# Hybrid decoder step on one core: a rest between the index groups, another first buffer for their relus, and a longer gap between attention's first loads and the values

## The chip, the core and the metric

The kernel runs on one core of a Trainium2 chip. The time is device time in microseconds (us) for one execution of the whole program, lower is better. TensorE (PE) does the matmuls, VectorE (DVE) and ScalarE (ACT) the element work, GpSimd (POOL) some element work and DMA issues, SyncE (SP) most DMA issues.

## What is computed

One step of a decoder layer for 1024 prompt tokens and 8 sample tokens: RMSNorm, one wide input projection, a sparse attention group (an index search picks 256 keys per query, attention then runs over these), an mLSTM group, and one output projection. The parts that the change touches are the index search and the attention over prompt tokens:

```python
def indexer_scores(qi, ki, wi):
    s = relu(einsum('bqhd,bld->bqlh', qi, ki))          # 16 heads of 64
    return einsum('bqlh,bqh->bql', s, wi) * IDX_SCALE

def block(args):                                         # one block of 128 queries
    scores = where(key_pos <= pos, indexer_scores(qib, ki, wib), -inf)
    _, idx = top_k(scores, 256)
    return sparse_attend(qb, k[idx], v[idx], idx <= pos)
```

## The kernel before

**Main work.** Nearly all of the span is a stream of projection matmuls on PE: first tile by tile (`mm`, L1596), then by a blocked scheme with fewer products (`product`, L1783; 48 matmuls of 258 columns each, every number split in a high and a low part so that three matmuls make one). Their inputs are weights that SP loads (L1768), ACT casts (L1771) and DVE subtracts (L1772), and partial sums that DVE evacuates (L1881) and SP stores and fetches (L1809, L1805).

**Side work.** The index search, attention, mLSTM and the sample tokens are generators ("jobs") in three lanes. Each `yield n` is n units of a job's weight. A lane hands its job's steps out evenly between the job's start and end (both in projection tiles; four clock steps make one), so a job's weight and a `yield` set the place of each step beside the projection, and a larger weight packs the other steps closer. A scheduler then puts the recorded instructions in an order on each engine by its own estimate of times; each engine runs its list in that order. The order is fixed when the program is built.

**Index search (`job_index`).** Query blocks 2 to 7 go in groups of two: (2,3), (4,5), (6,7). For each block and each of 16 heads PE makes scores (L483) in a PSUM bank, ACT applies the relu into one of three shared buffers "rl", "gt", "eq" (L486), and DVE adds the weighted relu to the block's sum s (L489; L497 and L499 for head 0). The buffers are taken in turn. Then a bit by bit search finds the 256th largest score (DVE L557 to L562, ACT L533, with gt and eq as scratch), and the mask is made in the same buffers: "gt" for the first block, "rl" for the second, with "eq" as scratch of both (L569 to L577). SP stores each mask to `biasS` (L578). A PSUM bank is free for another score when its relu is done; a buffer is free for a relu when DVE has read it and, if it held a mask, when the store has left it. At the border of two groups ACT, DVE, PE and SP so wait for each other in their own orders.

**Attention (`job_att`).** It opens its buffers in the space that the sample tokens' attention has left (its last store is L1438), loads the keys and the values (L605), the mask and the queries (L626, L628), rests for 15 units, transposes the values on PE (L613, eight transposes in two banks), splits values and queries (ACT L615, L633, DVE L616, L634), and then goes pair by pair through scores (L650), masked maximum (DVE L651), exp (ACT L667), transposes and values (L694, L703).

Of the kernel before, what the change touches and what calls it, by code (L numbers as in the profile page):

```python
# [42 lines left out]
T_AK = 9  # L43
T_AV = 11
T_AQ = 13
T_G = 21
# [131 lines left out]
def body(tc, A, stop=None):  # L178
# [270 lines left out]
    def job_index(groups):  # L449
        with tc.tile_pool(name="ix", bufs=2) as px:  # L450
# [4 lines left out]
            qv = qS.rearrange("(h p) r -> p h r", p=128)  # L455
            quads = [(i, h) for blocks in groups for i in blocks for h in range(0, 16, 4)]
            qis = {}
            ring, turn = ("rl", "gt", "eq"), [0]

            def load_q(n):  # L460
                if n < len(quads):
# [8 lines left out]
            yield 3000  # L470
            for blocks in groups:
                n = len(blocks)
                Sv = []
                for i in blocks:
                    W = (i + 1) * 128
# [88 lines left out]
                for q, i in enumerate(blocks):  # L564
                    W = (i + 1) * 128
                    gt = px.tile([128, S], BF16, name="rl" if q else "gt", bufs=1)
                    eq = px.tile([128, S], BF16, name="eq", bufs=1)
# [13 lines left out]
    def job_att():  # L581
        early.close()
        blocks = [(0, i) for i in range(7, -1, -1)] + [(1, i) for i in range(8)]
        pairs = [(g, i, hp) for g, i in blocks for hp in range(2)]
        with tc.tile_pool(name="at", bufs=2) as pa:
# [22 lines left out]
            def split_v(vt):  # L608
                vH, vL = (pa.tile([128, 8, 128], F32R, name=f"v{x}", bufs=1) for x in "HL")
                for b4 in range(2):  # L610
                    p = bank().rearrange("p (a b) -> p a b", a=4)
                    for j in range(4):
                        PE.transpose(p[:, j, :], vt[b4][:, j * 128:j * 128 + 128], ident)  # L613
                    bs = slice(b4 * 4, b4 * 4 + 4)
                    SC.copy(vH[:, bs], p)  # L615
                    V.tensor_tensor(vL[:, bs], p, vH[:, bs].bitcast(F32), OP.subtract)  # L616
                cur["v"] = vH, vL
                cur["rc"] = pa.tile([128, 4, 8], F32, name="rc", bufs=2)

            def load_q(g, i):  # L620
                W = (i + 1) * 128
                if i < 2:
                    bias = cmask[:, 256 - W:]
                else:
                    bias = pa.tile([128, S], BF16, name="bias", bufs=2)
                    SY.dma_start(bias[:, :W], biasS[i])  # L626
                q = pa.tile([128, 4, 128], F32R, name="qL", bufs=2)
                SY.dma_start(q.bitcast(F32), aqS[g].rearrange("(j p) r -> p j r", p=128)[:, :, i * 128:(i + 1) * 128])  # L628
                return q, bias
# [78 lines left out]
            split_k()  # L708
            vt = load_v(0)
            pre = load_q(*blocks[0])  # L710
            yield 15
            split_v(vt)
            split_q(*pre)
            pre = load_q(*blocks[1])
# [5 lines left out]
            for n, pair in enumerate(pairs):  # L720
                g, i, hp = pair
# [807 lines left out]
    def ix_weight(blocks):  # L1529
# [4 lines left out]
    groups = ((2, 3), (4, 5), (6, 7))  # L1534

    lanes = [Lane([Job("gates", 5, T_AK - 0.5, 14500, job_gates),
                   Job("index", T_AK + 2.1, 28.2, 6000 + sum(map(ix_weight, groups)), lambda: job_index(groups)),
                   Job("att", T_G + 17.8, 47.3, 2 * 2 * sum(2 * (1 + (i + 1) * 0.5) for i in range(8)) + 24, job_att, att_free),
                   Job("ml", T_G + 20, 55.8, 41, job_ml, lo_done)]),
             Lane([Job("prep", 3, T_AK + 1.8, 1 + 16 * 2, job_prep),  # L1540
                   Job("dscore", T_AK + 2.4, 17.9, 56 + 128 + 2, job_dscore),
# [593 lines left out]
    turn = [0]  # L2135
# [354 lines left out]
def build(arrays):  # L2490
    nc = bacc.Bacc("TRN2", target_bir_lowering=False, num_devices=1)
    A = {}
    for name, a in arrays.items():
        A[name] = nc.dram_tensor(f"in_{name}_dram", a.shape, mybir.dt.from_np(a.dtype), kind="ExternalInput").ap()
    for name, shape in OUTS.items():
        A[name] = nc.dram_tensor(f"out_{name}_dram", shape, F32, kind="ExternalOutput").ap()
    with tile.TileContext(nc, schedule_with_timeline_sim=True) as tc:
        body(tc, A)
    return nc
# [8 lines left out]
```

## Time and profile before

| | |
|---|---|
| median of 3 runs | 1910.79 us (1910.09 to 1913.55) |
| the profiled execution, its own time | 1910.03 us |
| its span, first to last instruction | 1908.2 us |
| PE busy | 1878.0 us, 98% of the span |
| weight load on PE | 1808.6 us, 95% |
| DVE busy | 1394.1 us, 73% |
| ACT busy | 915.0 us, 48% |
| POOL busy | 511.2 us, 27% |
| mean granted TensorE clock | 0.995 of full |

The profile is one execution. Busy times overlap, so that the span is about PE's busy time with PE's idle time. A line of the waits says which engine and line waited, for which engine and line, and gives the total, the number of times and the longest. A line of the timeline gives the start from the span's start, the length, the engine and line, the tiles, and in brackets the idle time before it with what ended it.

### The profile page before, as it was taken

The numbers are of one execution on the slowest core, as the hardware profiler recorded it, in microseconds if no ns is written. First come the engines' busy times: TensorE is split into PE (matmuls) and PEld (weight loads), VectorE is DVE, ScalarE is ACT, GpSimd is POOL, SyncE is SP. The second block draws the span as 40 slices with busy tenths as digits, with TensorE's granted clock in tenths as the row PEclk, the third lists the DMA queues.
The fourth block names the chain that finished last, engine by engine and source line by source line (L and its number), as shares of the span: only waits on it lengthen the run. The fifth ranks groups of instructions, "written<-read, shape, count | busy, mean of one in ns | idle before, by whom it ended". The sixth has DMA issues, their size and how long they took to land. (4 is left out here: it accounts for less than half of the span.)

```text
span 1908.2 us, 37435 instructions
## 1 busy us (share of the span) xinstructions
PE 1878.0 (98%) x13422; PEld 1808.6 (95%) x13422; DVE 1394.1 (73%) x3266; ACT 915.0 (48%) x1822; POOL 511.2 (27%) x600
## 2 busy tenths in 40 slices
PE   9999999999989999999999999999999999999998
PEld 8999999999989999999899999999999999987886
DVE  8564386776778988998566566558988676788786
ACT  8222145346445465522255555436656444454654
POOL 0599853320000011054111111102211241105541
PEclk9999999999999999999999999999999999999999
DMA  7577857757787798799977898688999979899797
GB/s 265 160 215 212 256 182 238 201 160 180 212 256 203 212 250 235 224 315 303 252 183 188 237 250 199 156 266 260 320 315 287 213 238 298 274 336 309 254 221 237
DMA packets 253703, 456.64 MB, mean 239 GB/s; under 512 B 38165, under 2 KB 113877, under 8 KB 249837
## 3 DMA queue, kind: packets, MB, share of 16 engines
q1 hardware_dynamic: 192445, 331.24, 53.5%
q0 software_dynamic: 27648, 102.34, 23.6%
q10 hardware_dynamic: 33424, 20.68, 3.6%
q8 instruction: 105, 1.72, 0.4%
q14 instruction: 81, 0.66, 0.1%
HBM read 363.72 MB, written 138.67 MB: 263 GB/s over the span
## 5 line engine op out<-in xcount | busy, mean ns | idle before, releaser
L1783 PE MATMUL pj<-xH 128*128 128x258 f32 x1920 | 546.7, 285 | 1.0 <-ACT mH L1581 1.0
L1783 PE MATMUL pj<-xL,xH 128*128 128x258 f32 x1920 | 546.0, 285 | 0.0
L1783 PE MATMUL pj<-xH,xL 128*128 128x258 f32 x1920 | 545.5, 285 | 0.0
L1783 PEld LDWEIGHTS pj<-xH 128*128 128x128 f32 x1920 | 363.7, 190 | 3.5 <-ACT mH L1581 1.4
L1783 PEld LDWEIGHTS pj<-xH,xL 128*128 128x128 f32 x1920 | 363.9, 190 | 1.7
L1783 PEld LDWEIGHTS pj<-xL,xH 128*128 128x128 f32 x1920 | 363.9, 190 | 1.5
L1596 PE MATMUL pj<-xH,wH 128*128 128x344 f32 (+1 forms) x816 | 265.3, 328 | 1.3 <-ACT xH L325 0.8
L1596 PE MATMUL pj<-xH,wL 128*128 128x344 f32 (+1 forms) x816 | 264.6, 325 | 0.5 <-DVE wL L269 0.5
L1596 PE MATMUL pj<-xL,wH 128*128 128x344 f32 (+1 forms) x816 | 264.5, 324 | 0.2 <-DVE xL L326 0.2
L269 DVE TENSOR_TENSOR wL<-wraw,wH 128x512 fp32r<-128x512 f32 (+2 forms) x151 | 117.4, 790 | 96.5 <-ACT wH L268 95.3
L268 ACT CAST wH<-wraw 128x512 fp32r<-128x512 f32 (+2 forms) x151 | 89.8, 607 | 181.8 <-PE pj L1596 102.5
L1596 PEld LDWEIGHTS pj<-xH,wH 128*128 128x128 f32 x816 | 153.0, 188 | 3.9 <-ACT xH L325 2.1
L1596 PEld LDWEIGHTS pj<-xL,wH 128*128 128x128 f32 x816 | 153.3, 188 | 1.1 <-DVE xL L326 0.7
L1596 PEld LDWEIGHTS pj<-xH,wL 128*128 128x128 f32 x816 | 153.3, 188 | 1.0 <-DVE wL L269 0.8
L2160 PE MATMUL pj<-wH,sH 128*128 128x512 f32 x336 | 131.8, 393 | 3.3 <-DVE yt L2278 2.9
L2160 PE MATMUL pj<-wH,sL 128*128 128x512 f32 x336 | 131.5, 391 | 0.0
L2160 PE MATMUL pj<-wL,sH 128*128 128x512 f32 x336 | 123.3, 392 | 0.5 <-DVE wL L2149 0.5
L1771 ACT CAST xH<-wH 128x1024 fp32r<-128x1024 f32 x91 | 75.9, 834 | 99.9 <-PE pj L1783 75.1
L1771 ACT CAST xH<-wL 128x1024 fp32r<-128x1024 f32 x91 | 76.1, 836 | 95.0 <-PE pj L1783 58.8
L1772 DVE TENSOR_TENSOR xL<-wH,xH 128x1024 fp32r<-128x1024 f32 x91 | 87.0, 956 | 15.6 <-ACT xH L1771 13.9
L1772 DVE TENSOR_TENSOR xL<-wL,xH 128x1024 fp32r<-128x1024 f32 x91 | 86.9, 955 | 11.4 <-ACT xH L1771 10.5
L1783 PE MATMUL bank<-xH 128*128 128x258 f32 x320 | 91.4, 286 | 0.0
(508 smaller groups left out, 4445.1 us busy)
## 6 DMA issues: line engine op xcount, KB each, us to landing
wraw<-in_wt_dram SPq DMA_DIRECT2D x144, 256.0 KB
usD<-in_wa_dram POOLq DMA_DIRECT2D x46, 512.0 KB, 7.8
wraw<-in_wa_dram SPq DMA_DIRECT2D x78, 256.0 KB
wraw<-in_wo_dram SPq DMA_DIRECT2D x64, 256.0 KB
usD<-in_wa_dram SPq DMA_DIRECT2D x26, 512.0 KB
wH<-in_wa_dram SPq DMA_DIRECT2D x25, 512.0 KB
wL<-in_wa_dram SPq DMA_DIRECT2D x24, 512.0 KB
spD<-ev SPq DMA_DIRECT2D x46, 258.0 KB
```

The lines of the kernel that those rows point to most:

```text
L268: a = paced("act", SC.copy(H[:, s, :cols], raw[:, s, :cols]))
L269: return a, V.tensor_tensor(L[:, s, :cols], raw[:, s, :cols], H[:, s, :cols].bitcast(F32), OP.subtract)
L1596: m = PE.matmul(ps[:cols, :cn], w_[:, k, :cols], x_[kk][:, c0:c0 + cn], start=(kk == ends[0] and z == 0), stop=(kk == ends[1] and z == 2))
L1771: paced("act", SC.copy(H[:, q], r))
L1772: paced("dve", V.tensor_tensor(L[:, q], r, H[:, q].bitcast(F32), OP.subtract))
L1783: PE.matmul(ps[c], w_[:, q, ks], x[y][:, c * CS:c * CS + CS], start=(first and q == 0 and k == 0 and z == 0), stop=(q == 1 and k == 3 and ...
L2160: PE.matmul(ps[b], S_[x][:, b * 128:b * 128 + 128], T_[y], start=(k == 0 and z == 0), stop=(k == 7 and z == 2))
```

## The change

It sets the turn of the relu buffers back to 0 at each group and turns their order to eq, gt, rl. It puts a rest of 7000 units ahead of the second and third group, and adds 14000 to the index job's weight. It makes the rest of attention between its first loads and the split of the values 24 units in place of 15, adds 9 to its weight, and moves its end from 47.3 to 47.5. No instruction of computation is added or taken away. The line numbers of the changed kernel are 3 higher from L475 on.

```diff
             quads = [(i, h) for blocks in groups for i in blocks for h in range(0, 16, 4)]
             qis = {}
-            ring, turn = ("rl", "gt", "eq"), [0]
+            ring, turn = ("eq", "gt", "rl"), [0]
...
             yield 3000
             for blocks in groups:
                 n = len(blocks)
+                turn[0] = 0
+                if blocks != groups[0]:
+                    yield 7000
                 Sv = []
...
             vt = load_v(0)
             pre = load_q(*blocks[0])
-            yield 15
+            yield 24
             split_v(vt)
...
-                   Job("index", T_AK + 2.1, 28.2, 6000 + sum(map(ix_weight, groups)), lambda: job_index(groups)),
-                   Job("att", T_G + 17.8, 47.3, 2 * 2 * sum(2 * (1 + (i + 1) * 0.5) for i in range(8)) + 24, job_att, att_free),
+                   Job("index", T_AK + 2.1, 28.2, 20000 + sum(map(ix_weight, groups)), lambda: job_index(groups)),
+                   Job("att", T_G + 17.8, 47.5, 2 * 2 * sum(2 * (1 + (i + 1) * 0.5) for i in range(8)) + 33, job_att, att_free),
```

**PE, start of the index search's third group.** In both programs the first four score tiles of the group stand some 200 projection matmuls earlier; these are the fifth and the sixth (bank is the PSUM bank, ki the index keys, qi the queries, the rest is projection). Before:

```order
L483 MATMUL bank<-ki_2323,qi 128x512
L483 MATMUL bank<-ki_2324,qi 128x512
L1783 MATMUL pj_5355<-xL,xH 128x258
L1783 MATMUL pj_5355<-xH,xL 128x258
L1783 MATMUL pj_5356<-xH 128x258
L483 MATMUL bank<-ki_2323,qi 128x384
L483 MATMUL bank<-ki_2324,qi 128x384
```

With the change:

```order
L486 MATMUL bank<-ki_2323,qi 128x512
L486 MATMUL bank<-ki_2324,qi 128x512
L1786 MATMUL pj_5356<-xL,xH 128x258
L1786 MATMUL pj_5356<-xH,xL 128x258
L1786 MATMUL pj_5356<-xH 128x258
L1786 MATMUL pj_5356<-xL,xH 128x258
L1786 MATMUL pj_5356<-xH,xL 128x258
L1786 MATMUL bank<-xH 128x258
L1786 MATMUL bank<-xL,xH 128x258
L486 MATMUL bank<-ki_2323,qi 128x384
L486 MATMUL bank<-ki_2324,qi 128x384
```

Counted in projection matmuls from the start of the program, the fifth tile stands after 2974 before and after 2983 with the change, the sixth after 2977 and after 2990. The first four stand after 2736 before, and after 2760 and 2784 (two each) with the change.

**SP, the stores of the second group's masks.** biasS_119 takes the mask of block 4 from gt, biasS_120 that of block 5 from rl; the other rows belong to the projection. Before:

```order
L1768 DMA wL<-in_wa_dram 128x1024
L578 DMA biasS_119<-gt 128x640
L1736 DMA xL<-xsD 128x516
L1768 DMA wH<-in_wa_dram 128x512
L1809 DMA spD<-ev 128x516
L1768 DMA wL<-in_wa_dram 128x512
L578 DMA biasS_120<-rl 128x768
```

With the change:

```order
L1771 DMA wL<-in_wa_dram 128x1024
L1739 DMA xL<-xsD 128x516
L1771 DMA wH<-in_wa_dram 128x512
L581 DMA biasS_119<-gt 128x640
L1812 DMA spD<-ev 128x516
L1771 DMA wL<-in_wa_dram 128x512
L581 DMA biasS_120<-rl 128x768
```

The store from gt has moved behind two loads of the projection; the one from rl stands where it stood.

**SP, attention's first loads.** attS is the last store of the sample tokens' attention, pP the buffers of the values. Before:

```order
L1438 DMA attS_107<-ot 128x4x8
L1438 DMA attS_108<-ot 128x4x8
L1768 DMA wH<-in_wa_dram 128x512
L605 DMA pP<-avS_101 128x512
L1809 DMA spD<-ev 128x516
L1805 DMA rstd<-spD 128x516
L1768 DMA wL<-in_wa_dram 128x512
L605 DMA pP<-avS_101 128x512
L626 DMA bias<-biasS_122 128x1024
L628 DMA qL<-aqS_104 128x4x128
```

With the change:

```order
L1441 DMA attS_107<-ot 128x4x8
L1441 DMA attS_108<-ot 128x4x8
L1812 DMA spD<-ev 128x516
L1808 DMA rstd<-spD 128x516
L608 DMA pP<-avS_101 128x512 x2
L1771 DMA wL<-in_wa_dram 128x1024
L629 DMA bias<-biasS_122 128x1024
L631 DMA qL<-aqS_104 128x4x128
```

The two loads of values now stand together and ahead of two weight loads that they followed, counting back from the 1024 wide wL. On PE the transposes of the values stand after 5736 and 5743 projection matmuls before (four each), and all eight after 5808 with the change. Attention's last value matmul stands after 7272 before and after 7296 with the change.

## Rows read from the trace of the kernel before

**Rows 1.** The page, part 1: busy us, share of the span, instructions.
```profile
PE 1878.0 (98%) x13422; PEld 1808.6 (95%) x13422; DVE 1394.1 (73%) x3266; ACT 915.0 (48%) x1822; POOL 511.2 (27%) x600
```

**Rows 2.** Waits of PE, whole span: total us, times, longest us.
```profile
PE bank L483 <- ACT gt L486: 5.6, 2, 4.8
PE pj L2160 <- DVE yt L2278: 2.9, 1, 2.9
PE bank L613 <- DMA pP<-avS: 2.4, 1, 2.4
```

**Rows 3.** Timeline of PE, third index group: start, length, instruction, idle before.
```profile
554.14 0.73 PE L483 MATMUL bank<-ki,qi 128*128 128x512 f32 x2 [1.54 <-ACT eq L486]
...
560.04 1.01 PE L483 MATMUL bank<-ki,qi 128*128 128x384 f32 x2 [4.80 <-ACT gt L486]
...
564.35 0.28 PE L1783 MATMUL bank<-xH 128*128 128x258 f32 x1
564.47 0.28 PE L1783 MATMUL bank<-xL,xH 128*128 128x258 f32 x1
```

**Rows 4.** Timeline of ACT, the same place.
```profile
553.49 0.60 ACT L486 ACTIVATE eq<-bank 128x512 f32<-128x512 f32 x1 [5.80 <-DVE rl L576]
559.49 0.49 ACT L486 ACTIVATE gt<-bank 128x384 f32<-128x384 f32 x1 [5.40 <-DMA biasS<-gt]
...
562.59 0.60 ACT L486 ACTIVATE rl<-bank 128x512 f32<-128x512 f32 x1 [0.31 <-DMA biasS<-rl]
```

**Rows 5.** Timeline of DVE, the masks of blocks 4 and 5.
```profile
547.58 0.32 DVE L577 TENSOR_SCALAR gt<-gt 128x640 bf16<-128x640 bf16 x1
...
552.85 0.55 DVE L576 TENSOR_TENSOR rl<-rl,eq 128x768 bf16<-128x768 bf16 x1
```

**Rows 6.** Timeline of SP's DMA queue, the same place.
```profile
547.68 0.33 SPq L1768 DMA_DIRECT2D wL<-in_wa_dram  x1
548.11 0.60 SPq L578 DMA_DIRECT2D biasS<-gt  x1
548.76 0.49 SPq L1736 DMA_DIRECT2D xL<-xsD  x1
549.35 0.41 SPq L1768 DMA_DIRECT2D wH<-in_wa_dram  x1
```

**Rows 7.** Windows: stretch, its us, busy by engine, PEclk, DMA share, GB/s.
```profile
550.00:555.00 5.00, 3.46 (x27) 3.17 (x25) 3.76 (x7) 0.60 (x1) 0.00 (x0) 1.00 1.05 279
555.00:560.00 5.00, 0.24 (x3) 0.03 (x1) 0.00 (x0) 0.49 (x1) 0.00 (x0) 0.73 0.93 320
560.00:564.20 4.20, 4.16 (x18) 4.17 (x19) 3.14 (x7) 2.36 (x4) 0.00 (x0) 0.50 0.37 112
```

**Rows 8.** DMA issues, whole span: count, KB each.
```profile
xL<-xsD SPq DMA_DIRECT2D x40, 258.0 KB
...
wH<-in_wa_dram SPq DMA_DIRECT2D x22, 256.0 KB
```

**Rows 9.** Timeline of PE, the transposes of attention's first values.
```profile
928.93 0.63 PE L613 MATMUL bank<-cst,pP 128*128 128x128 f32 x4 [0.94 <-DMA spD<-ev]
...
932.78 1.11 PE L613 MATMUL bank<-cst,pP 128*128 128x128 f32 x4 [2.39 <-DMA pP<-avS]
```

**Rows 10.** Windows, behind those transposes.
```profile
932.80:936.20 3.40, 3.40 (x16) 3.40 (x17) 0.82 (x2) 1.10 (x2) 0.63 (x1) 0.50 1.06 350
```

**Rows 11.** Timeline of SP's DMA queue, attention's first loads.
```profile
917.01 1.23 SPq L1438 DMA_DIRECT2D attS<-ot  x2
...
922.95 0.33 SPq L605 DMA_DIRECT2D pP<-avS  x1
...
925.98 0.91 SPq L605 DMA_DIRECT2D pP<-avS  x1
```

**Rows 12.** Waits of SP's DMA queue, 910 to 946 us.
```profile
SPq L605 <- DMA attS<-ot: 3.8, 2, 3.4
```

**Rows 13.** Windows: the stretch of attention.
```profile
937.00:1240.00 303.00, 302.28 (x2394) 295.24 (x2393) 188.50 (x513) 161.51 (x375) 35.43 (x41) 1.00 0.80 207
```

**Rows 14.** Windows: most of the third group's scores.
```profile
570.00:655.00 85.00, 85.00 (x622) 80.97 (x621) 75.92 (x158) 43.07 (x74) 7.58 (x11) 1.00 0.75 209
```

## Prediction, made before the changed kernel ran

> **What bounds the kernel.** I read the page's busy times first: PE is busy for 1878.0 us of a span of 1908.2 us, every other engine for 73% of it or less [rows 1]. So the bound is the stream of matmuls on PE, and the change neither adds to it nor takes from it. What an edit of order can win is PE's idle time, 30.2 us in all, and what idle time does to its clock. The waits of PE come next: the three longest lines are 5.6 us of index scores (L483) for a relu, 2.9 us in the output projection (L2160), and 2.4 us of attention's first transposes (L613) for a DMA [rows 2]. The change comes near the first and the third. The second lies far behind everything that moves, and I leave it as it is.
>
> At the third index group PE waits twice: 1.54 us until the relu into eq is done, and 4.80 us until the relu into gt is done [rows 3]. ACT shows why. The relu into eq began at 553.49, after DVE's last reading of eq in the mask of block 5; the relu into gt began at 559.49, when the store of block 4's mask had left gt [rows 4]. DVE had finished that mask by 547.9 [rows 5] and SP had issued its store at 548.11 [rows 6]: the store took 11.4 us, in a stretch in which the DMA engines were busy 93% of the time and more [rows 7]. The clock pays a second time. It was at full (2.4 GHz) before the wait, and 0.50 (1.2 GHz) from 560.0 to 564.2, in which PE was busy throughout [rows 7]: 4.2 us of work at half speed, 2.1 us lost. The place costs 1.54 + 4.80 + 2.1 = 8.4 us.
>
> At attention's start PE waits 0.94 us and then 2.39 us for the two loads of the values [rows 9], and runs the next 3.4 us at 0.50 [rows 10], 1.7 us lost. This place costs 0.94 + 2.39 + 1.7 = 5.0 us.
>
> **The change part by part: attention.** The loads were late because SP waited 3.4 us for the sample tokens' last store to leave the space [rows 12], issued the first load at 922.95 and the second at 925.98 [rows 11], and PE took them up 6.0 and 6.8 us after their issue [rows 9]. The rest of 24 units puts the transposes 72 and 65 projection matmuls later. One such matmul takes 0.12 us at full clock (from 564.35 to 564.47, [rows 3]), so that is 8.6 and 7.8 us. The loads themselves move forward in SP's order, together and ahead of two weight loads. The slack of over 7 us, against waits of 0.94 and 2.39 us, covers both, and without the waits I see no cause for the clock to fall there. I take -5.0 us; the ends are -3.3 (the clock falls anyway) and -5.0.
>
> What is queued behind them: SP still waits for the sample tokens' store, and now the 1024 wide weight load stands behind that wait. In the old order the 512 wide wL stood behind the same wait, 3.4 us [rows 12], and no wait of PE for a weight came of it; I cost this at nothing, covered by the weights already cast. If that cover were gone, it would cost the same 3.4 us.
>
> The rest of attention starts 72 matmuls later and ends 24 later, so it loses 48 x 0.12 = 5.8 us of some 300 us. In that stretch PE was busy 302.28 of 303 us and DVE 188.50, ACT 161.51 [rows 13]. DVE at 62% goes to some 63%; I cost this at nothing, with 0 and +5.8 as ends.
>
> **The index search.** The rest of 7000 of now 418,918 units is 1.14 of the 68.4 clock steps that the job has, and the other steps are packed 3.3% closer. At the second group it moves the first scores 36 projection matmuls back; Besides the 4.80 us only 0.8 us is left of that line's 5.6 [rows 2, 3], so that is worth nothing. At the third group it moves the first four score tiles by 24 and 48 matmuls. But these four wait in their banks in any case; PE stops at the fifth and the sixth, which need a bank back. Those move by 9 and 13 matmuls only.
>
> With the new turn the first relu goes into eq, the second into gt and the third into rl. The fifth tile then waits for the relu into eq, as before, behind the same reading of eq in block 5's mask, which ended at 553.4 [rows 5]. PE comes 9 x 0.12 = 1.1 us later, so of the 1.54 us some 0.5 us is left. The sixth tile waits for the relu into gt, **the same store as before**. If that store still left at 559.49, PE would have done 13 x 0.12 = 1.6 us more of its work by then, and the place would cost 1.6 us less. In the new order the store stands behind the loads of xL and wH, 258 and 256 KB [rows 8], which followed it before [rows 6]. At the 320 GB/s that the core moved there [rows 7] these 514 KB take 1.6 us. That gives back the whole gain. I take 0 for this part. The ends are -1.6, and +1.5: the gt store as late as the rl store, whose relu began at 562.59 [rows 4], which is 3.1 us later, less the 1.6.
>
> Here a rule of the Trainium skill speaks against the edit. The rows show only issue and release, 548.11 and 559.49 [rows 4, 6]. DMA: Bandwidth & Descriptors, section "Queues, rings and completion order", says that each DMA engine takes the descriptors of one queue in ring order. By that rule the store can't pass the two loads that now precede it, and the sum below holds; without it the sum would be 1.6 us lower. The trace doesn't contradict it: the relu into rl, whose store was issued later, was released later too. No run here isolates it.
>
> **Sum.** The profiled execution took 1910.03 us, 1.83 us of it outside its span. Less 5.0 for attention and 0 for the index search that is 1905.0 us. The median of the runs, 1910.79, lies 0.76 us above that execution, so I forecast 1905.8 us.
>
> **The rivals.** 0.2%, 3.8 us, is about what a measurement of this kernel can tell from no change; the bounds are 1907.0 and 1914.6 us.
>
> *Both places are cured.* The rest could hold the critical tiles back until the stores have left, or the stores could leave sooner because less is under way beside them. For it: the waits are named in the rows and the rest stands in front of just these scores. Against it: the tiles that stop PE move by about one us, where the store would have to come over 4 us earlier. It would give 1905.8 - 8.4 = 1897.4 us.
>
> *The index wait grows, or a new wait takes its place.* DMA was full, and the new order puts more in front of the store. At the upper end the store costs +1.5 us, and with another 3.4 us at half clock 1.7 us more: 1905.8 + 3.2 = 1909.0 us, no change to speak of. The same holds for one new wait of that size elsewhere, since most of the order of side work has moved by some matmuls.
>
> *Slower: DVE becomes the bound of the scores.* The rest takes its time from the other steps, and the scores come 3.3% closer. In the third group's scores DVE was already busy 75.92 of 85 us, 89% [rows 14]. Should DVE fall behind, relus wait for their buffers, scores for banks and PE for the scores. For the two groups behind a rest, at 85 us each, the price is 3.3% of 170 us, 5.6 us of waiting, and a fall of the clock at 1.7 us in each: 1905.8 + 9.0 = 1914.8 us. It decides from the point where 89% becomes 100%; 3.3% more makes 92%, so the rows speak against it, though not for each short stretch.
>
> *The rest doesn't rest.* The order already shows this in part: the critical tiles hardly move. That is my forecast.
>
> **How the numbers follow.** The forecast (attention gains, index search doesn't) has 0.51, with a range of its own from 1903.5 to 1909; of it 0.36 is below 1907.0 and 0.15 between the bounds. Both cured has 0.19, all of it faster. The grown or new wait has 0.17: 0.02 faster, 0.13 the same, 0.02 slower. DVE as the bound has 0.13: 0.02 the same, 0.11 slower. Together 0.57 faster, 0.30 the same, 0.13 slower. The range reaches from 1896.5, which takes in both cured, to 1912.0, which takes in the grown wait and leaves most of the slower case out.
>
> **What would show it.** Right: no wait of L613 for the pP load (L616 in the new numbering), and full clock behind the eight transposes; at the third group PE still stops at the sixth score tile for the relu into gt, which is released by the store to biasS, for 4 to 7 us in all, with a stretch at 0.50 behind it. Wrong: that wait gone or below 2 us (both cured); waits of index scores for relus that wait for DVE (the slower case); a wait in attention's scores or values, or a clock below full in its stretch, that was not there before.

## The result, and the profile after

The changed kernel is **slower by 0.6%**: its ratio to the kernel before is 1.006, with a 95% interval from 1.0044 to 1.0076. The medians of seven runs each are 1925.36 us (1919.28 to 1930.32) and 1911.51 us (1910.09 to 1916.29). The forecast of 1905.8 us had the wrong sign, and the range up to 1912.0 us did not hold the result.

The profiled execution of the changed kernel took 1921.77 us, 1920.0 us of it its span. The page's busy times and the longest waits of PE, with total, times and longest, answer to [rows 1] and [rows 2]; lines of the changed kernel are 3 higher:

```profile
PE 1881.3 (98%) x13422; PEld 1812.5 (94%) x13422; DVE 1389.1 (72%) x3266; ACT 912.2 (48%) x1822; POOL 510.1 (27%) x600
```

```profile
PE bank L914 <- ACT qH L850: 5.4, 3, 2.9
PE bank L486 <- ACT gt L489: 4.1, 2, 3.8
PE pj L1786 <- DVE ev L1884: 3.3, 1, 3.3
```

PE's idle time rose from 30.2 to 38.7 us, 8.5 of the 11.8 us by which the spans differ; the rest is longer busy time. The wait for the values is gone, and of the three longest lines two are new: L914 are the matmuls of the mLSTM, which neither the prediction nor a rival had spoken of, and L1786 with "ev" is a projection that waits for an evacuation. L486 is the index search's wait of before.

**Where the time went.** The windows of the mLSTM's stretch, 1250 to 1570 us, before and after (us, busy time of PE, PEld, DVE, ACT, POOL, then PEclk, DMA share, GB/s):

```profile
1250.00:1570.00 320.00, 318.72 (x2672) 318.00 (x2672) 253.71 (x746) 173.71 (x380) 70.78 (x144) 1.00 0.89 274
```

```profile
1250.00:1570.00 320.00, 312.13 (x2608) 310.38 (x2608) 245.16 (x730) 169.62 (x376) 69.53 (x138) 1.00 0.87 271
```

PE is idle there for 1.3 us before and 7.9 us after: 6.6 of the 8.5 us. The last matmul of the mLSTM (L947) ends at 1512.3 us before and at 1522.6 us after; up to 1525 us the idle time is 0.3 and 6.2 us, and the rest lies behind the mLSTM. The longest wait is told by four engines. First SP's queue, ACT, DVE and PE of the changed kernel (start, length, instruction, idle before it):

```profile
1329.44 0.42 SPq L1255 DMA_DIRECT2D Cb<-in_sC_dram  x1
...
1331.39 1.02 SPq L1255 DMA_DIRECT2D Cb<-in_sC_dram  x1
```

```profile
1337.46 0.51 ACT L1266 ACTIVATE Cb<-Cb,w 128x256 f32<-128x256 f32 x1 [4.41 <-DMA Cb<-in_sC_dram]
...
1341.02 0.41 ACT L850 CAST qH<-d 128x256 fp32r<-128x256 f32 x1
```

```profile
1338.00 0.61 DVE L1268 SCALAR_TENSOR_TENSOR Cb<-wraw,dec,Cb 128x128 f32<-128x128 f32 x2 [5.74 <-ACT Cb L1266]
```

```profile
1341.48 0.39 PE L914 MATMUL bank<-CH,qH 128*128 128x258 f32 x1 [2.85 <-ACT qH L850]
```

Cb is the state of the sample tokens' mLSTM, another job in another lane. ACT came to its first scale 3.6 us after the load was issued (1337.46 less 4.41 is 1333.05, the load 1329.44) and stood for 4.41 us. Behind it in ACT's order stand the casts of the prompt tokens' mLSTM, and behind these PE. In the kernel before, ACT came to the same scale 7.1 us after the issue and did not wait:

```profile
1333.88 0.42 SPq L1252 DMA_DIRECT2D Cb<-in_sC_dram  x1
```

```profile
1340.96 0.90 ACT L1263 ACTIVATE Cb<-Cb,w 128x256 f32<-128x256 f32 x2
...
1342.53 0.41 ACT L847 CAST qH<-d 128x256 fp32r<-128x256 f32 x1
```

Here qH was ready at 1342.94 us, and the matmul that reads it began at 1345.72 without a wait:

```profile
1345.72 0.28 PE L911 MATMUL bank<-CH,qH 128*128 128x258 f32 x1
```

**Attention's start.** ACT, DVE and PE of the changed kernel, and the window around it:

```profile
930.19 0.62 ACT L636 CAST qH<-qL 128x512 fp32r<-128x512 f32 x1 [7.71 <-DMA qL<-aqS]
```

```profile
930.84 0.69 DVE L637 TENSOR_TENSOR qL<-qL,qH 128x512 fp32r<-128x512 f32 x1 [7.55 <-ACT qH L636]
931.45 0.75 DVE L1884 TENSOR_TENSOR ev<-pj,ev 128x258 f32<-128x258 f32 x2
```

```profile
931.92 0.58 PE L1786 MATMUL pj<-xH 128*128 128x258 f32 x1 [3.32 <-DVE ev L1884]
944.49 1.04 PE L616 MATMUL bank<-cst,pP 128*128 128x128 f32 x8
```

```profile
930.50:937.40 6.90, 5.48 (x25) 5.48 (x26) 3.10 (x5) 1.78 (x3) 0.85 (x1) 0.51 1.07 293
```

The values' transposes (944.49) no longer wait. But the split of the queries, which the program writes behind that of the values, now stands ahead of the transposes on ACT and DVE. It waits for its load, and the evacuation that PE needs stands behind it on DVE. PE waits 3.32 us and then works at 0.51 of its clock for 5.48 us, 2.7 us lost: 6.0 us in place of the 5.0 us of [rows 9, 10]. In a second profile of the changed kernel ("the change, second time" below) this wait was 2.0 us and the clock stayed at full, and PE waited another 1.5 us at attention's scores (L653). So the wait belongs to the order, but its size and the fall of the clock differ between executions. One of the signs that the prediction named for being wrong, a wait in attention's scores or values, came too, and is small: 1.8 us at L706 in the first profile.

**The index search.** PE at the third group:

```profile
554.76 0.73 PE L486 MATMUL bank<-ki,qi 128*128 128x512 f32 x2 [0.55 <-ACT eq L489]
560.17 1.01 PE L486 MATMUL bank<-ki,qi 128*128 128x384 f32 x2 [3.83 <-ACT gt L489]
```

It stops at the same two tiles as in [rows 3], for 4.4 us in place of 6.3.

### The profile page after: what moved, and what is told of

It reads as the page before. It is cut to its first block, busy times and chain, and to the rows that moved or that the text cites. A ratio compares the mean times of both kernels' runs of the same rounds, so it can differ in the third digit from the quotient of the medians.

```text
span 1920.0 us, 37413 instructions
## 1 busy us (share of the span) xinstructions
PE 1881.3 (98%) x13422; PEld 1812.5 (94%) x13422; DVE 1389.1 (72%) x3266; ACT 912.2 (48%) x1822; POOL 510.1 (27%) x600
## 5 line engine op out<-in xcount | busy, mean ns | idle before, releaser
L1786 PE MATMUL pj<-xH 128*128 128x258 f32 x1920 | 546.9, 285 | 6.2 <-DVE ev L1884 3.3
L1786 PE MATMUL pj<-xL,xH 128*128 128x258 f32 x1920 | 546.4, 285 | 0.8 <-issue 0.8
L1786 PE MATMUL pj<-xH,xL 128*128 128x258 f32 x1920 | 545.3, 285 | 0.1
L1786 PEld LDWEIGHTS pj<-xH 128*128 128x128 f32 x1920 | 364.1, 190 | 9.1 <-DVE ev L1884 3.5
L1786 PEld LDWEIGHTS pj<-xH,xL 128*128 128x128 f32 x1920 | 363.9, 190 | 2.5 <-issue 0.9
L1786 PEld LDWEIGHTS pj<-xL,xH 128*128 128x128 f32 x1920 | 364.2, 190 | 2.0 <-issue 0.5
L1786 PE MATMUL bank<-xH,xL 128*128 128x258 f32 x320 | 91.6, 286 | 0.0
```

The source lines that it names most:

```text
L1786: PE.matmul(ps[c], w_[:, q, ks], x[y][:, c * CS:c * CS + CS], start=(first and q == 0 and k == 0 and z == 0), stop=(q == 1 and k == 3 and ...
```

## Experiments

**Theory:** attention's end moved from 47.3 to 47.5, the mLSTM follows attention in the same lane, and its steps now stand where loads of other jobs are late. **Rivals:** the index edits cost it; or the new wait at attention's start and attention's closer steps do.

Each kernel was timed in turns with the kernel before on the same chip. The idle time of PE from 1250 to 1570 us is 320 us less the busy time in that row of its windows, and that up to 1525 us is 275 us less the busy time from 1250 to 1525 us. All matmuls of the mLSTM are done by 1525 us in every profile, so that the last column is the mLSTM's own. Each profile is one execution.

| kernel | ratio to before | 95% interval | PE idle, 1250 to 1570 us | of it up to 1525 us |
|---|---|---|---|---|
| the change | 1.0060 | 1.0044 to 1.0076 | 7.9 us | 6.2 us |
| the change, second time | 1.0072 | 1.0054 to 1.0090 | 11.5 us | 9.1 us |
| index edits alone | 0.9999 | 0.9981 to 1.0017 | 3.9 us | 0.0 us |
| attention edits alone | 1.0049 | 1.0032 to 1.0066 | 6.9 us | 5.0 us |
| attention's end 47.5 alone | 1.0042 | 1.0020 to 1.0064 | 6.9 us | 6.9 us |
| attention's rest of 24 alone | 1.0002 | 0.9983 to 1.0022 | 2.6 us | 0.3 us |
| end 47.1 | 1.0046 | 1.0025 to 1.0067 | 5.0 us | 5.0 us |
| end 47.4 | 1.0020 | 1.0004 to 1.0036 | 5.3 us | 5.3 us |
| end 47.5, mLSTM's end moved along | 1.0017 | 1.0002 to 1.0033 | 2.8 us | 2.8 us |
| rest of 24, queries split behind | 0.9995 | 0.9979 to 1.0011 | 7.0 us | 3.4 us |
| the same and the index edits | 1.0010 | 0.9995 to 1.0025 | 6.1 us | 4.3 us |
| rest inside attention | 0.9996 and 0.9997 | 0.9980 to 1.0012, 0.9983 to 1.0011 | 4.8 and 5.8 us | 3.1 and 1.8 us |
| the same and the index edits | 1.0006 | 0.9994 to 1.0018 | 5.2 us | 1.9 us |
| before, once more | 0.9993 | 0.9975 to 1.0010 | 0.9 us | 0.6 us |
| the change, mLSTM put back | 1.0014 | 0.9999 to 1.0030 | 5.3 us | 3.2 us |
| before, mLSTM moved | 1.0053 | 1.0034 to 1.0072 | 8.7 us | 3.4 us |

### Which edit costs

The index edits alone:

```diff
-ring, turn = ("rl", "gt", "eq"), [0]
+ring, turn = ("eq", "gt", "rl"), [0]
+                turn[0] = 0
+                if blocks != groups[0]:
+                    yield 7000
-Job("index", T_AK + 2.1, 28.2, 6000 + ...
+Job("index", T_AK + 2.1, 28.2, 20000 + ...
```

> Only the index edits (new turn of the relu buffers, reset, the two rests of 7000). Theory (the loss lies in the mLSTM stretch and comes from the attention edit): -2 us against before, 1907 to 1911, since the changed kernel's trace has 1.9 us less idle time of PE between 545 and 600 us and no other new wait in the first half. Rival (the closer scores or the new turn cost time in the first half): 4 us or more above before. Rival (the changed kernel's start is slower for a reason of its own, its clock reached full 8.1 us later and its 200th projection matmul came 2.2 us later): +0 to +1, and the late clock seen again.

0.9999: no cost and no gain shows, with an interval of some 3.5 us to either side, so that the 2 us of the theory are neither shown nor ruled out.

The attention edits alone:

```diff
-            yield 15
+            yield 24
-Job("att", T_G + 17.8, 47.3, ... + 24, job_att, att_free)
+Job("att", T_G + 17.8, 47.5, ... + 33, job_att, att_free)
```

> Only the attention edits (rest of 24, weight, end 47.5). Theory: the whole loss is here, 10 to 14 us above before, in the mLSTM stretch 6 us or more of PE's waits for the split q (the line qH in the mLSTM prep), behind a wait of ACT for the load of Cb of over 4 us; at attention's start the wait of 3.3 us for the evacuation is there again. Rival (index edits cost it): within 2 us of before.

1.0049, some 9 us: most of the loss, if a little under the expected 10 to 14. ACT waited 4.1 us for Cb and PE 2.69 us for qH, as in the changed kernel; at attention's start the wait came at another evacuation ("rstd", 2.7 us).

Attention's end alone:

```diff
-Job("att", T_G + 17.8, 47.3, ...
+Job("att", T_G + 17.8, 47.5, ...
```

> Only attention's end, 47.5 in place of 47.3; its rest stays at 15. Its attention starts as in before, its mLSTM matmuls stand where the changed kernel has them, but on ACT the first scale of Cb stands after 146 weight casts as in before, where the changed kernel has it after 143. Theory A (mLSTM runs late because its steps start later and are packed closer): 5 to 10 us above before, waits of PE for qH. Theory B (the loss is ACT waiting for Cb ahead of the q split, which needs both shifts): within 2 us of before, no wait of PE for qH over 1 us.

1.0042, some 8 us, in the range of theory A. Theory B, that all hangs on ACT's wait for Cb ahead of qH, falls: no wait for qH is left, and the time is lost all the same. But the waits for qH were theory A's sign as well, and did not come. ACT and PE near the mLSTM's end:

```profile
1511.48 0.39 ACTq L950 DMA_DIRECT2D hS<-hT  x1
1511.97 0.62 ACT L1771 CAST xH<-wL 128x512 fp32r<-128x512 f32 x1 [11.21 <-DMA xH<-spD]
```

```profile
1518.00 0.69 PE L947 MATMUL bank<-cst,hm 128*128 128x128 f32 x2 [6.62 <-ACT hm L939]
```

Another load is late in another order: ACT stands still for 11.21 us ahead of a weight cast, which the profile puts down to a load of the projection's partial sums (spD). The store hS of the mLSTM, which precedes that cast in ACT's order, was issued only at the end of this wait. The mLSTM's last transposes wait for what is behind it.

Attention's rest alone:

```diff
-            yield 15
+            yield 24
-... + 24, job_att, att_free)
+... + 33, job_att, att_free)
```

> Only attention's rest of 24 and its weight; its end stays at 47.3, and from the mLSTM on the order is that of before. Theory (the loss is in the mLSTM stretch): within 3 us of before; at the start of attention the wait for the values (2.4 us) is gone, and a wait for an evacuation that stands behind the split of the queries on DVE may have taken its place, with half clock behind it. Rival (the new wait at attention's start and its half clock, or the closer steps of attention, carry the loss): 5 us or more above before.

1.0002, as the theory has it. In one point the expectation was wrong: the mLSTM's first groups (L911) do not stand as in before, but after 7419 projection matmuls in place of 7440. So this shift, 21 earlier, costs nothing that shows. ACT, DVE and PE show the exchange of waits again:

```profile
936.18 0.62 ACT L633 CAST qH<-qL 128x512 fp32r<-128x512 f32 x1 [7.35 <-DMA qL<-aqS]
```

```profile
936.83 0.69 DVE L634 TENSOR_TENSOR qL<-qL,qH 128x512 fp32r<-128x512 f32 x1 [6.66 <-ACT qH L633]
```

```profile
937.92 0.58 PE L1783 MATMUL pj<-xH 128*128 128x258 f32 x1 [2.94 <-DVE rstd L1881]
```

### Later, closer, or out of place

The end moved the other way:

```diff
-Job("att", T_G + 17.8, 47.3, ...
+Job("att", T_G + 17.8, 47.1, ...
```

> Before with attention's end moved the other way, 47.1 in place of 47.3. The mLSTM's first group stands after 7392 projection matmuls (before 7440, attention's end at 47.5 7456). Theory A (the mLSTM comes too late and is packed too closely when attention ends later): an earlier end gives it more room, so 0 to 8 us faster than before, at the least not slower. Theory C (before's phase of the mLSTM against its neighbours' loads, stores and the sample tokens' mLSTM is a good spot, and a shift to either side costs): 3 to 10 us slower, with waits of PE in the mLSTM stretch.

1.0046: an end that puts the mLSTM's first groups 48 matmuls earlier costs as much as one that puts them 16 later. Theory A falls as it was put. The mLSTM's waits in this stretch:

```profile
PE bank L911 <- ACT qH L847: 2.5, 2, 2.1
PE bank L947 <- ACT hm L939: 1.3, 1, 1.3
PE bank L875 <- DMA rb<-rowS: 1.3, 1, 1.3
```

Half the move:

```diff
-Job("att", T_G + 17.8, 47.3, ...
+Job("att", T_G + 17.8, 47.4, ...
```

> Before with attention's end at 47.4, half the move of the change. The mLSTM's first groups stand as in before (7440 projection matmuls), the sample tokens' Cb scales up to one or two weight casts earlier on ACT. Theory C (before stands on a good spot of the mLSTM against its neighbours): 2 to 8 us slower. Theory A (later is worse): a cost between 0 and that of 47.5, about 4 us.

1.0020, within what both theories allow. With the run above that speaks for theory C, but not for every shift: with the rest alone the first groups stand 21 matmuls earlier, with the queries' split kept behind (below) 9 earlier, and neither cost shows. Here the first groups did not move at all, and the wait is again behind Cb: its first scale stands one weight cast earlier on ACT, which waits 7.44 us for the load, and PE 4.21 us for the copy hT behind it:

```profile
1340.30 0.91 ACT L1263 ACTIVATE Cb<-Cb,w 128x256 f32<-128x256 f32 x2 [7.44 <-DMA Cb<-in_sC_dram]
```

```profile
1341.73 1.12 PE L880 MATMUL bank<-cst,qkv 128*128 128x128 f32 x4 [4.21 <-ACT hT L949]
```

The mLSTM's end moved along:

```diff
-Job("att", T_G + 17.8, 47.3, ...
-Job("ml", T_G + 20, 55.8, 41, job_ml, lo_done)
+Job("att", T_G + 17.8, 47.5, ...
+Job("ml", T_G + 20, 56.0, 41, job_ml, lo_done)
```

> Attention's end at 47.5 as in the changed kernel, and the mLSTM's end moved by the same 0.2, from 55.8 to 56.0, so that its steps have the spacing of before and only come later. Theory A1 (the closer packing costs): within 2 us of before. Theory A2 (coming later costs, in front of loads and casts that stand in the way): 5 to 10 us slower, as with the end alone.

1.0017, some 3.2 us, between A1's bound and A2's; its interval, 0.4 to 6.3 us, reaches into both. Closer packing may be a part of the cost, but while the mLSTM's first groups stand where the end alone has them, its later steps stand elsewhere, so the run doesn't show which.

### The mLSTM's place alone

The changed kernel with the mLSTM put back, and the kernel before with it moved:

```diff
             for _ in range(5):
-                yield 1
+                yield 0.7600
-Job("ml", T_G + 20, 55.8, 41, job_ml, lo_done)
+Job("ml", T_G + 20, 55.8, 39.8, job_ml, lo_done)
```

> The changed kernel, with the mLSTM's first rest shortened by 1.2 of its 41 units (five steps of 0.76 in place of 1). From the mLSTM's first matmul on, PE and ACT then have the order of before, DVE and SP but for 4 and 3 rows; all that comes earlier is as in the changed kernel. Theory (the mLSTM's place carries the loss, index edits and attention's start give nothing): within 3 us of before, 7 to 9 us faster than the changed kernel beside it. Rival (the loss hangs on what attention and the index search do ahead of it, and the mLSTM stretch is only where it shows): as slow as the changed kernel, 6 us or more above before.

```diff
             for _ in range(5):
-                yield 1
+                yield 1.2400
-Job("ml", T_G + 20, 55.8, 41, job_ml, lo_done)
+Job("ml", T_G + 20, 55.8, 42.2, job_ml, lo_done)
```

> The kernel before, with the mLSTM's first rest lengthened by 1.2 units (five steps of 1.24) and nothing else. From the mLSTM's first matmul on, the order is that of the changed kernel but for 24 rows on PE, 2 on ACT, 20 on DVE and 10 on SP; all that comes earlier is as in before. Theory: the whole loss, 7 to 11 us above before, with waits of PE for the split q in the mLSTM stretch. Rival: within 3 us of before.

The changed kernel beside them:

> The changed kernel once more, beside the two others on one chip: 7 to 11 us above before; in its second profile PE idle for 6 us or more from 1250 to 1570 us again, with waits for the split q of the mLSTM and an ACT wait for Cb ahead of them. Rival (the waits of the first profile were chance): less than 3 us idle there.

Of the changed kernel's 0.72% on this chip, moving the mLSTM alone makes 0.53%, and with the mLSTM put back 0.14% is left, which can't be told from nothing. The two add up to 0.67%. **The place of the mLSTM carries most of the loss**, by the times of both kernels. The waits for Cb and for qH came again with its order, 4.33 and 2.73 us in the kernel before with the mLSTM moved, 4.70 and 3.58 us in the changed kernel. With the mLSTM put back ACT came to Cb without a wait. ACT and PE of the kernel before with the mLSTM moved, and its clock behind that wait:

```profile
1328.24 0.91 ACT L1263 ACTIVATE Cb<-Cb,w 128x256 f32<-128x256 f32 x2 [4.33 <-DMA Cb<-in_sC_dram]
```

```profile
1332.99 0.41 PE L911 MATMUL bank<-CH,qH 128*128 128x258 f32 x1 [2.73 <-ACT qH L847]
```

```profile
1333.20:1336.60 3.40, 3.40 (x17) 3.40 (x17) 3.40 (x8) 1.62 (x3) 0.00 (x0) 0.50 0.86 213
```

The profiles show only a part of the 10 us. In the mLSTM this kernel has 3.4 us of idle PE and 3.4 us at half clock, 1.7 us lost; the kernel with the mLSTM put back has 3.2 us of idle PE there too. Of the 8.7 us in the table 5.3 lie behind the mLSTM's last matmul, in one wait for an evacuation. There its order is that of before, and the index edits alone, whose order there is the same as well, have 3.9 us at the same place, where the two profiles of before have none of it:

```profile
PE pj L1783 <- DVE rstd L1881: 5.2, 1, 5.2
```

```profile
PE pj L1786 <- DVE rstd L1884: 3.9, 1, 3.9
```

The rest inside attention, one kernel in two executions, has 0.9 and 3.4 us there. So this wait differs between executions of one order, and how much of it the mLSTM's place brings about is not shown.

The same stretch of the kernel before, once more:

> The kernel before, once more with a profile, to see how much of PE's waits changes from one execution to another with the order unchanged. If the mLSTM stretch (1250 to 1570 us) of before is quiet by its order, PE is idle there for 1 to 4 us again (1.3 us in the first profile, 3.9 us in the run of the index edits, whose order there is the same); if that was chance, 5 us and more as in the changed kernel.

```profile
1250.00:1570.00 320.00, 319.09 (x2675) 318.46 (x2675) 254.46 (x747) 173.00 (x381) 71.23 (x145) 1.00 0.90 274
```

Quiet again, 0.9 us. Kernels with its order in this stretch and another one ahead of it have 3.9 to 5.8 us there (the index edits, the mLSTM put back, the rest inside attention), but a part of that lies behind the mLSTM. Up to 1525 us it is 0.0 us with the index edits and 1.8 to 3.2 us with the others, against 2.8 to 9.1 us in the kernels whose mLSTM or Cb was moved by attention's end or by the mLSTM's rest. So before is quiet in two executions of two, but the order in this stretch alone does not make it so. Why it doesn't stays open.

### What attention's start is worth

The queries' split kept behind the values', on ACT and DVE:

```diff
-            def split_q(q, bias):
+            def split_q(q, bias, keep=lambda m: m):
...
-                SC.copy(qH, q.bitcast(F32))
-                V.tensor_tensor(q, q.bitcast(F32), qH.bitcast(F32), OP.subtract)
+                keep(SC.copy(qH, q.bitcast(F32)))
+                keep(V.tensor_tensor(q, q.bitcast(F32), qH.bitcast(F32), OP.subtract))
...
-            yield 15
+            yield 24
             split_v(vt)
-            split_q(*pre)
+            split_q(*pre, pin)
...
-... + 24, job_att, att_free)
+... + 33, job_att, att_free)
```

> Attention's rest of 24 with its end at 47.3, and the first split of the queries kept behind the split of the values on ACT and DVE, where the program writes it (the scheduler had put it 10 us and more ahead). Theory (the gain at attention's start was taken back by the queries' split, on which ACT waited 7.35 us for its load and DVE 6.66 us, with an evacuation behind it): no wait of PE over 1 us between 925 and 950 us, full clock there, 4 to 5 us faster than the rest alone, so 1911 to 1914 beside a before of 1917. Rival (yet another wait takes that place, or the waiting was not on the path): within 1.5 us of the rest alone.

Its windows from 915 to 960 us, and from 1250 to 1570 us:

```profile
915.00:960.00 45.00, 45.00 (x352) 43.59 (x351) 27.54 (x62) 19.25 (x37) 6.88 (x8) 1.00 1.01 288
```

```profile
1250.00:1570.00 320.00, 312.97 (x2608) 312.03 (x2607) 252.70 (x741) 172.47 (x379) 68.99 (x144) 0.99 0.87 269
```

The start is cured: PE is busy all 45 us, at full clock, where before it was idle for 3.3 us. But PE is then idle for 7.0 us from 1250 to 1570 us, 5.7 more than before, 3.1 of it in the mLSTM and the rest behind it, and the ratio is 0.9995. The mLSTM's first groups stand 9 projection matmuls earlier than in before.

The same with the index edits:

> The index edits of the change, the rest of 24 with the end at 47.3, and the queries' split kept behind the values'. Theory (the index edits give nothing, the start of attention 4 to 5 us): 4 to 5 us faster than before. Rival (the two don't add up): within 1.5 us of before.

1.0010, so no gain is added by them.

The mLSTM held in its place, the rest lengthened at the cost of attention's first pair:

```diff
-            yield 15
+            yield 22
...
-                yield cost[n]
+                yield cost[n] - (3.5 if n == 0 else 0)
...
-                yield cost[n]
+                yield cost[n] - (3.5 if n == 0 else 0)
```

with the queries' split kept behind as above.

> The rest ahead of attention's values is 22 in place of 15, the 7 units are taken from attention's first pair (two steps of 5 become 1.5 each), its weight and end stay as in before, and the first split of the queries is kept behind that of the values. From the mLSTM's first matmul on, PE and ACT have the order of before, so the mLSTM is held in its place. Theory (attention's start is worth the 5.0 us of the prediction, and the mLSTM's place took them back): 4 to 5 us faster than before, no wait of PE over 1 us from 870 to 960 us, and the mLSTM's waits as in before. Rival (the start is not worth anything, a later stretch takes it back whatever the order there): within 1.5 us of before.

> The longer rest inside attention with the queries' split behind the values' once more, since its profile showed the start cured and a span 5 us shorter than the two profiles of before, but its 12 times only 0.04% less, with an interval of 0.3%. If the cure of attention's start reaches the end: 2 to 5 us faster. If it is taken back in the mLSTM stretch: within 1.5 us of before, PE idle there for 4 us and more again.

0.9996 and 0.9997. In both profiles the start is cured. The spans are 1903.4 and 1913.8 us, on chips on which the runs of before had medians of 1909.75 and 1918.93 us; their middle is lower by 2.45 and 1.45 us. By the ratios 0.8 and 0.6 us are left of the 5.0, and the intervals, from 3.8 us faster to 2.3 us slower, include none. From 1250 to 1570 us PE is idle for 4.8 and 5.8 us, before for 1.3 and 0.9; 3.1 and 1.8 us of it lie in the mLSTM, the rest behind it. That the mLSTM took the gain back is so not shown: the first of the two profiles has a span 5 us shorter than those of before, and the times do not bear it out. Where the gain goes stays open.

With the index edits:

> The same with the index edits of the change. Theory (index edits 0, start of attention 4 to 5 us): 4 to 6 us faster than before. Rival (the index edits cost or gain on their own): over 2 us off the run without them.

1.0006. No version here beats the kernel before by more than its interval.

## Why the prediction was wrong

**The step that failed** is "The rest of attention starts 72 matmuls later and ends 24 later [...] I cost this at nothing". It looked at attention's own stretch only. The lane hands its next job the time at which attention ends, so the mLSTM's first matmuls (L875) moved by 24 projection matmuls, from 7392 to 7416, and its first groups (L911) by 16, from 7440 to 7456, against the casts, loads and stores of the projection. The sample tokens' mLSTM, in another lane, did not keep its place either: its first matmuls (L1232) stand after 7661 in place of 7736, and its first scale of Cb on ACT after 143 weight casts in place of 146. The same holds when the mLSTM alone is moved, and that cost 0.53%, some 10 us, where the sum had 0. Of these the trace shows the wait for Cb, the wait for qH behind it and the half clock; where the rest is lost stays open. The prediction had seen that the end moved, and asked about the work that moves closer together, not about the work that comes next.

**A second step failed in its size**: "-5.0 us" at attention's start. The wait for the values went as it was worked out, and the eight transposes ran without one. But "What is queued behind them" was asked of SP alone. On ACT and DVE the queries' split had stood between the two splits of the values, where its wait for the load fell beside PE's own for the values; it now stands first. That order is fixed when the program is built, so it could have been read before the run. What took the place cost 3.3 us of waiting and 2.7 us of clock in the first profile, and the rest alone came out at 1.0002. "I see no cause for the clock to fall there" fell with it. Nor did the 5.0 us come where the start was cured: PE was busy throughout from 915 to 960 us, and the ratios were 0.9995 to 0.9997. The reading of [rows 9] was also too free: the profile puts the first wait, 0.94 us, down to a store of the projection (spD) and not to a load of the values, and the second profile of before has only the second wait, 2.7 us.

**The index search was right**, as a term of 0: 0.9999 alone. PE stopped at the fifth and the sixth tile, for eq and for gt, for 4.4 us in all, within the forecast 4 to 7 us. That this is 1.9 us less than before shows no gain: the kernel before, once more, stopped there for 0.40 and 3.58 us, 4.0 us, and the changed kernel in its second profile for 5.5 us. ACT's relu into gt was released by the same store:

```profile
559.63 0.49 ACT L489 ACTIVATE gt<-bank 128x384 f32<-128x384 f32 x1 [4.92 <-DMA biasS<-gt]
```

It came at 559.63, before at 559.49 [rows 4], though the store was issued 1.2 us later (549.29 and 548.11). Whether ring order took its 1.6 us is not decided by that: with the old order, the second profile of before had PE released 1.6 us sooner than the first (560.04, [rows 3]):

```profile
558.40 1.01 PE L483 MATMUL bank<-ki,qi 128*128 128x384 f32 x2 [3.58 <-ACT gt L486]
```

DMA: Bandwidth & Descriptors of the Trainium skill, section "Queues, rings and completion order", has descriptors taken in ring order on each DMA engine, but says as well that a later one may finish its write before an earlier one. So the prediction's "can't pass" says more than that section does.

**The rivals.** The slower rival had the right sign for a reason that did not come: from 600 to 800 us, the third group's scores, PE was idle for 0.00 us in the changed kernel. "A new wait takes its place" was right as a mechanism, twice, and priced as one wait of 3.2 us. It was several, at the start of attention and in the mLSTM, and the chance of slower, 0.13, was too small for a change that moves most of the order of the side work.

**The clock and the chips.** Times of one kernel differ by more than the effects here: before ran from 1900.99 to 1918.36 us on one chip. Only ratios to runs beside them are compared above.

## What to carry to other kernels

When a job's end or weight is changed, follow the job that comes after it in the same lane, and the jobs of other lanes that stand beside that one: an end that put the mLSTM's first groups 16 matmuls later or 48 earlier cost 0.4 to 0.5%, 8 to 9 us, more than the 5.0 us of the wait that the edit was near to, while 9 and 21 earlier, in kernels whose start of attention had changed too, cost nothing that showed. When a wait for a load is removed from one engine, list for every engine what is queued around it and on which load it waits, since the next late load takes its place, with the clock's fall. And profile the kernel before a second time: what its own order does in two executions tells which waits belong to the order. Before a wait is put down to a job, check that it lies in that job: here a good part of the idle time in the mLSTM's stretch stood behind its last matmul.

## What was not expected of the hardware

PE stood still near 880 us for reasons that no engine gives, in pieces of 0.2 to 1.0 us put to "issue", 2.0 us in the changed kernel and 3.1 us with attention's end alone, whose order up to there is that of before. The second profile of the changed kernel, with the same order, has none of it. The windows from 880 to 885 us with attention's end alone and of the kernel before, once more:

```profile
880.00:885.00 5.00, 1.93 (x10) 1.42 (x8) 1.34 (x3) 0.00 (x0) 2.74 (x3) 0.94 0.97 311
```

```profile
880.00:885.00 5.00, 5.00 (x44) 5.00 (x43) 4.29 (x6) 0.13 (x1) 3.87 (x4) 1.00 0.99 359
```

Runtime: NRT & Kernel Launch of the Trainium skill, section "Instruction fetch mechanics", says that an engine's sequencer fetches its instructions by a DMA queue of its own, and that this is mostly hidden. Whether a late fetch makes these gaps no run here shows; the DMA share is 0.97 and 0.99.

The start differs between executions as well. From 8 to 12 us PE was busy throughout before and after, and did 25 matmuls in the one and 14 in the other:

```profile
8.00:12.00 4.00, 4.00 (x25) 3.89 (x24) 2.63 (x5) 4.00 (x8) 0.00 (x0) 1.00 0.37 140
```

```profile
8.00:12.00 4.00, 4.00 (x14) 4.00 (x14) 2.85 (x6) 4.00 (x7) 0.00 (x0) 1.00 0.35 136
```

That is PE at about half its rate for some microseconds longer. The granted clock of both rows is 1.00, so it doesn't tell why. The 200th projection matmul came 2.2 us later, which is a part of the longer span of the profiled execution and not of the change: the order there is the same.
